# Two LayerNorms of a decoder layer: normalising on ScalarE, the bias on GpSimd, sums from the residual

## The chip, the core and the metric

The kernel runs on one core of a Trainium2 chip. It computes one whole decoder layer for 2048 tokens of width 1024 in one launch. The metric is the device time of an execution in microseconds (us). The engines of the core are TensorE (PE; PEld is its loading of weights), VectorE (DVE), ScalarE (ACT), GpSimd (POOL) and SyncE (SP), which issues most transfers.

## What is computed

The layer has two sub-layers: a token mixer of three head groups, and a mixture of experts (64 routed experts, eight for a token, and one shared expert). Behind each of them the residual stream is normalised; these two norms are what the change touches:

```python
def layer_norm(x, g, b):
    xf = x.astype(jnp.float32)
    mu = xf.mean(-1, keepdims=True)
    var = jnp.square(xf - mu).mean(-1, keepdims=True)
    return ((xf - mu) * lax.rsqrt(var + LN_EPS)).astype(x.dtype) * g + b

# each sub-layer:  x <- LayerNorm(ALPHA * x + gate * sublayer(x * (1 + scale) + shift))
```

All is float32, and the 2048 tokens are 16 blocks of 128 rows, a block's rows on the 128 partitions and its 1024 features along them.

## The kernel before

The input projection and the mixers, with the modulation rows, take up to about 1800 us of the profile. Then `phase_c` multiplies the mixers' output by the output projection and makes the **first norm**, a block of 128 rows at a time, and routes tokens to experts. The last phase, `moe_phase`, runs the experts; its end makes the **last norm** and writes the result. A scheduler lays out each engine's instructions, by the order of the code, priorities and its own estimates of durations, so that the code of several blocks is interleaved on every engine; what stands first in an engine's row waits for its inputs, and what is behind it waits as well.

**The first norm.** `tile_` (L1818) has five steps for each of the 16 blocks, and the loop over `t` advances three blocks in turn. For each half of 512 columns PE makes `po` (L1836), and VectorE makes the residual `r = ALPHA * x + po` (L1837) and takes `bn_stats` of it (L1840). `layer_norm_hat` (L1988) joins the two halves with `bn_aggr` (L1996), adds epsilon (L1998), takes the inverse root in `rsqrt` (L711 to L716: 11 tiny operations of VectorE, each reading the one before it) and makes the bias `lnnb` (L2001). ScalarE then normalises `r` in place (L2004). VectorE makes from it `h` and `h2p`, the experts' input (L1845, L1849), and the scaled residual (L1851, L1852). PE transposes `h2p` (L1860) and makes the router's scores (L1865). `route` (L1869) selects experts for the scores of four blocks at a time, of two at the very end; GpSimd's queue writes its gates `gt` (L1925) and counts (L1942). Both are small operations of VectorE. After the last block `rank_experts` (L1681) makes the tables that the experts need.

**The last norm.** In the last stage, from about 3620 us, the ten shared-expert units of `finish` (L2353) go one after the other: PE makes `py` (L2126, L2129), VectorE adds it to `a`, which is the routed experts' sum times the gate row (L2350), and takes the row sums `lnsu` with it (L2371). The six blocks whose shared-expert part was made earlier, SH0 = 6 (L1660), are mixed in between and get their sum on VectorE alone (L2366). Two blocks at a time then go through `norm` (L2320): the negative mean (L2327), squares and their sum on ScalarE (L2329), variance (L2332), `rsqrt`, and for each block two operations of VectorE over 128x1024, `(y + mean) * ln_g` (L2339) and `y * rs + ln_b` (L2340). Then SP sends the block out (L2341). The last block goes in two halves. `norm` is a generator, and `norms` (L2312) advances those under way before each unit. GpSimd has nothing to do in this stage.

Of the kernel before, what the change touches and what calls it, by code (L numbers as in the profile page):

```python
# [6 lines left out]
F32 = mybir.dt.float32  # L7
# [5 lines left out]
AF = mybir.ActivationFunctionType  # L13
ALU = mybir.AluOpType
AX = mybir.AxisListType
PSUM = bass.MemoryType.PSUM
P = 128
T = 2048
D = 1024
# [9 lines left out]
ALPHA = 2.0 ** 0.25  # L29
# [673 lines left out]
def rsqrt(nc, pool, x, shape, floor=None, name="rs"):  # L703

    V = nc.vector
    if floor is not None:
        V.tensor_scalar(x, x, floor, None, op0=ALU.max)
    t = pool.tile(shape, I32, name=name + "i")
    y = pool.tile(shape, F32, name=name + "y")
    a = pool.tile(shape, F32, name=name + "a")  # L710
    V.tensor_scalar(t, x.bitcast(I32), 1, None, op0=ALU.logical_shift_right)  # L711
    V.tensor_scalar(y.bitcast(I32), t, -1.0, float(0x5f3759df), op0=ALU.mult, op1=ALU.add)  # L712
    for _ in range(3):
        V.scalar_tensor_tensor(a, y, -0.5, y, op0=ALU.mult, op1=ALU.mult)  # L714
        V.tensor_tensor(a, a, x, op=ALU.mult)  # L715
        V.scalar_tensor_tensor(y, a, 1.5, y, op0=ALU.add, op1=ALU.mult)  # L716
    return y
# [1037 lines left out]
def phase_c(tc, A, g, S, mixT, modrow, C):  # L1755


    nc = tc.nc
    V, G, ACT, PE = nc.vector, nc.gpsimd, nc.scalar, nc.tensor
    woH, woL = C.wo  # L1760
    with ExitStack() as es:
# [3 lines left out]
        wk = pool("c_wk", 2)  # L1765
# [52 lines left out]
        def tile_(t, h2T):  # L1818
            t0 = t * P
            parts = C.first if t == 0 else []  # L1820
            load = mixed(nc, S, mx_ if t % 2 else C.mx, t, parts, G if t == 1 else nc.sync, V)
            if t:
                next(load)
            x = xp.tile([P, D], F32, name="x")
            nc.sync.dma_start(x, A["x"][0, t0:t0 + P, :])
            if t:
                next(load)
            mH, mL = parts
            yield
            r = rp.tile([P, D], F32, name="r")  # L1830
            for n in range(2):
                ps = C.pp.tile([P, CH], F32, name="po")
                sl = slice(n * 512, (n + 1) * 512)
                for k in range(KT):
                    for i, (a_, b_) in enumerate(((mH, woH), (mH, woL), (mL, woH))):
                        PE.matmul(ps, lhsT=a_[:, k, :], rhs=b_[:, k, sl], start=(k == 0 and i == 0), stop=(k == KT - 1 and i == 2))  # L1836
                V.scalar_tensor_tensor(r[:, sl], x[:, sl], ALPHA, ps, op0=ALU.mult, op1=ALU.add)  # L1837
                if n == 0:
                    st = sm.tile([P, 2, 6], F32, name="lnst", bufs=2)
                V.bn_stats(out=st[:, n, :], in_=r[:, sl])  # L1840
                yield
            xh = layer_norm_hat(tc, sm, r, r, st=st)
            yield
            h2 = wk.tile([P, D], F32, name="h2")
            V.tensor_tensor(h2, xh, bc["sc2"], op=ALU.mult)  # L1845

            hp = wk.tile([P, D], F32, name="h2p", bufs=3)
            cut = lambda a: a.rearrange("p (q k) -> p q k", k=KT)
            V.tensor_tensor(hp.rearrange("p (k q) -> p q k", k=KT), cut(h2), cut(bc["sh2"]), op=ALU.add)  # L1849
            h2 = hp  # L1850
            V.tensor_tensor(xh, xh, lng, op=ALU.mult)  # L1851
            V.tensor_tensor(xh, xh, lnb, op=ALU.add)  # L1852
            nc.sync.dma_start(S["x1"][t0:t0 + P, :], xh)
            nc.sync.dma_start(S["h2"][t0:t0 + P, 0:D], h2)
            yield
            hT = wk.tile([P, KT, P], F32, name="hT")
            for n in range(2):
                ps = pt.tile([P, CH], F32, name="tr")
                for k in range(4):
                    PE.transpose(ps[:, k * P:(k + 1) * P], h2[:, (4 * n + k) * P:(4 * n + k + 1) * P], g.ident)  # L1860
                ACT.activation(hT[:, 4 * n:4 * n + 4, :].rearrange("p a b -> p (a b)"), ps, AF.Copy)
            yield
            ps = pr.tile([P, CH], F32, name="rt")
            for k in range(KT):
                PE.matmul(ps[:, 0:NE], lhsT=hT[:, k, :], rhs=rw[:, k, :], start=(k == 0), stop=(k == KT - 1))  # L1865
            ACT.activation(h2T, ps[:, 0:NE], AF.Sigmoid)
            yield
# [117 lines left out]
        rank_experts(tc, g, S, cnt_e, sm, pr)  # L1985


def layer_norm_hat(tc, sm, out, r, parts=1, st=None):  # L1988

    nc = tc.nc  # L1990
    if st is None:
        st = sm.tile([P, 2, 6], F32, name="lnst")
        for n in range(2):
            nc.vector.bn_stats(out=st[:, n, :], in_=r[:, n * 512:(n + 1) * 512])
    mv = sm.tile([P, 2], F32, name="lnmv")
    nc.vector.bn_aggr(out=mv, in_=st)  # L1996
    va = sm.tile([P, 1], F32, name="lnva")
    nc.vector.tensor_scalar(va, mv[:, 1:2], 1e-5, None, op0=ALU.add)  # L1998
    y = rsqrt(nc, sm, va, [P, 1], None, "ln")
    nb = sm.tile([P, 1], F32, name="lnnb")  # L2000
    nc.vector.scalar_tensor_tensor(nb, mv[:, 0:1], -1.0, y, op0=ALU.mult, op1=ALU.mult)  # L2001
    for i in range(parts):
        c = slice(i * D // parts, (i + 1) * D // parts)
        nc.scalar.activation(out[:, c], r[:, c], AF.Identity, bias=nb, scale=y)  # L2004
    return out
NEAR = 4
NEAR2 = 5
# [6 lines left out]
def moe_phase(tc, A, g, S, modrow, out):  # L2014
    nc = tc.nc
    V, G, ACT, PE = nc.vector, nc.gpsimd, nc.scalar, nc.tensor
    with ExitStack() as es:
# [302 lines left out]
        def norm(blocks):  # L2320


            n = len(blocks)
            mean = sm.tile([P, 2], F32, name="lnmean")[:, 0:n]
            sq = sm.tile([P, 2], F32, name="lnsq")[:, 0:n]
            for i, (rows, y, su) in enumerate(blocks):
                V.tensor_scalar(mean[:, i:i + 1], su[:, 0:1], su[:, 1:2], -1.0 / D, op0=ALU.add, op1=ALU.mult)  # L2327
                junk = xg.tile([P, HC], F32, name="x")[:, 0:D]
                ACT.activation(junk, y, AF.Square, bias=mean[:, i:i + 1], accum_out=sq[:, i:i + 1])  # L2329
            yield  # L2330
            va = sm.tile([P, 2], F32, name="lnva")[:, 0:n]
            V.tensor_scalar(va, sq, 1.0 / D, 1e-5, op0=ALU.mult, op1=ALU.add)  # L2332
            rs = rsqrt(nc, sm, va, [P, n], None, f"ln{n}")
            yield
            for i, (rows, y, su) in enumerate(blocks):
                parts = 2 if rows.stop == T else 1
                for q in range(parts):
                    hs = slice(q * D // parts, (q + 1) * D // parts)
                    V.scalar_tensor_tensor(y[:, hs], y[:, hs], mean[:, i:i + 1], ln[0][:, hs], op0=ALU.add, op1=ALU.mult)  # L2339
                    V.scalar_tensor_tensor(y[:, hs], y[:, hs], rs[:, i:i + 1], ln[1][:, hs], op0=ALU.mult, op1=ALU.add)  # L2340
                    nc.sync.dma_start(out[rows, hs], y[:, hs])  # L2341
                yield

# [150 lines left out]
```

## Time and profile before

| what | us |
|---|---|
| time of the runs, median of 3 | 3731.58 (3721.93 to 3741.07) |
| the profiled execution | 3729.63 |
| its span, first to last instruction | 3727.9 |
| PE busy | 3439.3 (92%) |
| VectorE busy | 2640.9 (71%) |
| ScalarE busy | 1962.2 (53%) |
| GpSimd busy | 881.8 (24%) |

The shares are means over the whole span. What an edit is worth is read in its own stage, from the busy time in that stretch and from the wait that ends last there. The names behind a line are the tile written, an arrow, and the tiles read; the tile `w` in the last norm is the block `y`, and `wraw` is the row `ln_g` or `ln_b`, both kept in buffers that weights used earlier. In the first norm the norm's tiles are called `lnmv`, `lnva`, `lny`, `lnnb`.

### The profile page before, as it was taken

What the parts mean: (1) busy time and instruction counts of PE and PEld (TensorE: products, weight loads), DVE (VectorE), ACT (ScalarE), POOL (GpSimd) and SP (SyncE); (2) the same over time, 40 slices, a digit from 0 to 9 for tenths busy, and PEclk for the clock granted to TensorE, in tenths of its full rate; (3) what the DMA queues carried; (4) which work ended last, traced back from release to release, by engine and by line L of the source; (5) the groups of instructions that cost most, each with busy time, mean ns of one, the idle gap of its engine ahead of it and who ended that gap; (6) DMA issues with size and microseconds to landing.
All of it is one profiled execution on the core that took longest, in us unless ns stands there. A gap on an engine that the chain in (4) does not pass through costs nothing. (4 is left out here: it accounts for less than half of the span.)

```text
span 3727.9 us, 64046 instructions
## 1 busy us (share of the span) xinstructions
PE 3439.3 (92%) x23084; PEld 2985.7 (80%) x23084; DVE 2640.9 (71%) x6951; ACT 1962.2 (53%) x3471; POOL 881.8 (24%) x817
## 2 busy tenths in 40 slices
PE   7899999799999879999898799999999999999998
PEld 5677777688888767778787798998888888888996
DVE  6555899888888678888799545555556555556659
ACT  4243656355555567767322355555555555556642
POOL 1000000322223155543000022332223322232210
PEclk9999999899999889999999899999999999999999
DMA  7756466400000132222543478888889888888986
GB/s 251 232 199 221 150 211 226 162 26 25 20 24 18 30 105 79 84 66 78 170 149 140 146 206 232 242 232 233 244 244 242 244 236 234 236 234 256 290 237 215
DMA packets 276235, 640.38 MB, mean 172 GB/s; under 512 B 34428, under 2 KB 115364, under 8 KB 275784
## 3 DMA queue, kind: packets, MB, share of 16 engines
q1 hardware_dynamic: 231760, 481.09, 38.6%
q0 software_dynamic: 40832, 150.32, 18.2%
q10 hardware_dynamic: 3320, 4.83, 0.4%
q8 instruction: 183, 3.00, 0.3%
q14 instruction: 140, 1.15, 0.1%
HBM read 467.14 MB, written 169.00 MB: 171 GB/s over the span
## 5 line engine op out<-in xcount | busy, mean ns | idle before, releaser
L2112 PE MATMUL p<-hH,w 128*128 128x256 f32 (+8 forms) x4352 | 875.1, 289 | 9.3 <-DVE w L2060 6.6
L2112 PEld LDWEIGHTS p<-hH,w 128*128 128x128 f32 x4352 | 707.4, 191 | 18.9 <-DVE w L2060 6.9
L2060 DVE TENSOR_TENSOR w<-wraw,w 128x1024 fp32r<-128x1024 f32 x396 | 474.7, 1223 | 293.2 <-ACT w L2059 278.9
L2112 PE MATMUL p<-hL,w 128*128 128x256 f32 (+8 forms) x2176 | 617.2, 284 | 0.7 <-DVE hL L65 0.7
L2059 ACT ACTIVATE w<-wraw 128x1024 fp32r<-128x1024 f32 x396 | 406.2, 1054 | 234.5 <-DMA wraw<-in_exp_w_dram 112.2
L2166 POOL DMA_INDIRECT scratch_acc<-y,idx x157 | 262.3, 1671 | 782.6 <-ACT y L2165 312.8
L2129 PE MATMUL py<-w,gH 128*128 128x512 f32 (+5 forms) x1384 | 441.8, 401 | 2.0 <-ACT gH L62 1.6
L2112 PEld LDWEIGHTS p<-hL,w 128*128 128x128 f32 x2176 | 416.4, 191 | 6.5 <-DVE hL L65 0.9
L343 PE MATMUL pj<-hTH,w 128*128 128x512 f32 x1152 | 376.6, 402 | 16.6 <-ACT w L202 10.8
L65 DVE TENSOR_TENSOR hL<-tr,hH 128x512 fp32r<-128x512 f32 (+7 forms) x346 | 213.2, 627 | 210.8 <-ACT hH L62 197.6
L2129 PEld LDWEIGHTS py<-w,gH 128*128 128x128 f32 (+5 forms) x1384 | 236.6, 178 | 68.4 <-issue 8.1
L2165 ACT ACTIVATE y<-py,gt 128x512 f32<-128x512 f32 (+5 forms) x314 | 213.6, 683 | 145.9 <-PE py L2129 132.8
L343 PEld LDWEIGHTS pj<-hTH,w 128*128 128x128 f32 x1152 | 220.5, 193 | 70.8 <-ACT w L202 13.8
L62 ACT ACTIVATE hH<-tr 128x512 fp32r<-128x512 f32 (+7 forms) x346 | 184.3, 545 | 176.1 <-PE tr L2072 156.5
L2129 PE MATMUL py<-w,gL 128*128 128x512 f32 (+5 forms) x692 | 273.9, 396 | 0.6 <-DVE gL L65 0.5
L2140 POOL DMA_INDIRECT x<-scratch_h,idx x157 | 162.9, 1038 | 333.0 <-DVE L L2182 80.3
L343 PE MATMUL pj<-hTL,w 128*128 128x512 f32 x576 | 230.9, 401 | 0.0
L2072 PE MATMUL tr<-ident,x 128*128 128x128 f32 (+5 forms) x1384 | 191.9, 265 | 35.0 <-issue 17.9
L2072 PEld LDWEIGHTS tr<-ident,x 128*128 128x128 f32 (+5 forms) x1384 | 149.6, 140 | 46.0 <-issue 30.5
L2129 PEld LDWEIGHTS py<-w,gL 128*128 128x128 f32 (+5 forms) x692 | 122.9, 178 | 39.1 <-DVE gL L65 1.8
L2093 PE MATMUL p<-w,hH 128*128 128x256 f32 (+2 forms) x736 | 141.8, 289 | 0.0
L343 PEld LDWEIGHTS pj<-hTL,w 128*128 128x128 f32 x576 | 111.5, 194 | 23.5 <-issue 0.9
(626 smaller groups left out, 8152.0 us busy)
## 6 DMA issues: line engine op xcount, KB each, us to landing
wraw<-in_exp_w_dram SPq DMA_DIRECT2D x384, 512.0 KB
w<-scratch_wH SPq DMA_DIRECT2D x57, 512.0 KB
w<-scratch_wL SPq DMA_DIRECT2D x57, 512.0 KB
mw<-in_w_mod_dram SPq DMA_DIRECT2D x48, 512.0 KB
scratch_rw<-po SPq DMA_DIRECT2D x44, 256.0 KB
w<-in_w_in_dram SPq DMA_DIRECT2D x21, 512.0 KB
x<-in_x_dram SPq DMA_DIRECT2D x40, 256.0 KB
scratch_wH<-w SPq DMA_DIRECT2D x19, 512.0 KB
```

The lines of the kernel that those rows point to most:

```text
L62: nc.scalar.activation(hi, src, AF.Copy)
L65: (lo_eng or nc.vector).tensor_tensor(lo, src, hi.bitcast(F32), op=ALU.subtract)
L343: nc.tensor.matmul(ps, lhsT=a_[:, k, :], rhs=b_[k], start=(k == 0 and i == 0), stop=(k == KT - 1 and i == 2))
L2059: ACT.activation(wh[:, c], raw, AF.Copy)
L2060: V.tensor_tensor(wl[:, c], raw, wh[:, c].bitcast(F32), op=ALU.subtract)
L2072: PE.transpose(ps[:, k * n:(k + 1) * n], x[0:n, (4 * h + k) * P:(4 * h + k + 1) * P], g.ident[0:n, 0:n])
L2093: PE.matmul(ps[i][:n, 0:256], lhsT=(hH, hL)[a][:, k, 0:n], rhs=w[i][b][:, k, :], start=(k == 0 and j == 0), stop=(k == KT - 1 and j == 2))
L2112: PE.matmul(ps[i][:, 0:n], lhsT=w[i][a][:, k, m * P:(m + 1) * P], rhs=(hH, hL)[b][:, k, 0:n], start=(k == 0 and j == 0), stop=(k == KT - 1 ...
L2129: PE.matmul(ps[:n], lhsT=(gH, gL)[a][:, m, c:c + n], rhs=w[2][b][:, m, h * CH:(h + 1) * CH], start=(more is None and m == 0 and j == 0), s ...
L2140: G.indirect_dma_start(out=x[0:m, :], out_offset=None, in_=S["h2"], in_offset=bass.IndirectOffsetOnAxis(ap=ix[0:m], axis=0))
L2165: ACT.activation(y[:m, hs], ps[:m], AF.Copy, scale=gt[:m])
L2166: G.indirect_dma_start(out=S["acc"], out_offset=bass.IndirectOffsetOnAxis(ap=ix[0:m], axis=0), in_=y[0:m, :], in_offset=None, compute_op=A ...
```

## The change

In the first norm the two `bn_stats` and the `bn_aggr` of a block go. The residual's operation on VectorE now accumulates the row sum of each half (`accum_out`), one tiny operation makes the negative mean, and ScalarE squares the centred block with accumulation; the squares themselves go into the tile `h2`, which is overwritten later. The normalising by ScalarE stays.

In the last norm a tiny operation makes `nb = mean * rs` for the two blocks. ScalarE then normalises the block in place, VectorE multiplies by `ln_g`, and `ln_b` is added by GpSimd for blocks 0 to 13 and by VectorE for the last two. The transfer out waits for the addition.

```diff
@@ tile_
-                V.scalar_tensor_tensor(r[:, sl], x[:, sl], ALPHA, ps, op0=ALU.mult, op1=ALU.add)
                 if n == 0:
-                    st = sm.tile([P, 2, 6], F32, name="lnst", bufs=2)
-                V.bn_stats(out=st[:, n, :], in_=r[:, sl])
+                    su = sm.tile([P, 2], F32, name="lnsu", bufs=2)
+                V.scalar_tensor_tensor(r[:, sl], x[:, sl], ALPHA, ps, op0=ALU.mult, op1=ALU.add, accum_out=su[:, n:n + 1])
                 yield
-            xh = layer_norm_hat(tc, sm, r, r, st=st)
-            yield
             h2 = wk.tile([P, D], F32, name="h2")
+            xh = layer_norm_hat(tc, sm, r, r, su, h2)
+            yield
             V.tensor_tensor(h2, xh, bc["sc2"], op=ALU.mult)
@@ layer_norm_hat
-    nc.vector.bn_aggr(out=mv, in_=st)
+    nc.vector.tensor_scalar(mean, su[:, 0:1], su[:, 1:2], -1.0 / D, op0=ALU.add, op1=ALU.mult)
     va = sm.tile([P, 1], F32, name="lnva")
-    nc.vector.tensor_scalar(va, mv[:, 1:2], 1e-5, None, op0=ALU.add)
+    nc.scalar.activation(junk, r, AF.Square, bias=mean, accum_out=va)
+    nc.vector.tensor_scalar(va, va, 1.0 / D, 1e-5, op0=ALU.mult, op1=ALU.add)
     y = rsqrt(nc, sm, va, [P, 1], None, "ln")
     nb = sm.tile([P, 1], F32, name="lnnb")
-    nc.vector.scalar_tensor_tensor(nb, mv[:, 0:1], -1.0, y, op0=ALU.mult, op1=ALU.mult)
+    nc.vector.tensor_tensor(nb, mean, y, op=ALU.mult)
@@ norm
             rs = rsqrt(nc, sm, va, [P, n], None, f"ln{n}")
+            nb = sm.tile([P, 2], F32, name="lnnb")[:, 0:n]
+            V.tensor_tensor(nb, mean, rs, op=ALU.mult)
             yield
             for i, (rows, y, su) in enumerate(blocks):
+                ACT.activation(y, y, AF.Identity, bias=nb[:, i:i + 1], scale=rs[:, i:i + 1])
+                ended = rows.stop > T - 2 * P
                 parts = 2 if rows.stop == T else 1
                 for q in range(parts):
                     hs = slice(q * D // parts, (q + 1) * D // parts)
-                    V.scalar_tensor_tensor(y[:, hs], y[:, hs], mean[:, i:i + 1], ln[0][:, hs], op0=ALU.add, op1=ALU.mult)
-                    V.scalar_tensor_tensor(y[:, hs], y[:, hs], rs[:, i:i + 1], ln[1][:, hs], op0=ALU.mult, op1=ALU.add)
+                    V.tensor_tensor(y[:, hs], y[:, hs], ln[0][:, hs], op=ALU.mult)
+                    (V if ended else G).tensor_tensor(y[:, hs], y[:, hs], ln[1][:, hs], op=ALU.add)
                     nc.sync.dma_start(out[rows, hs], y[:, hs])
```

The scheduler also lays the instructions out anew. Two places follow. The first is VectorE in the last stage, near its end: before, the two passes of the last norm (L2339, L2340) over two blocks, beside the sums (L2371) of the next one.

```order
L2327 TENSOR_SCALAR lnmean<-lnsu 128x1
L2340 SCALAR_TENSOR_TENSOR w<-w,ln2y,wraw 128x1024 x2
L2332 TENSOR_SCALAR lnva<-lnsq 128x2
L2339 SCALAR_TENSOR_TENSOR w<-w,lnmean,wraw 128x1024
L2350 TENSOR_TENSOR x<-x,g2b 128x1024
L711 TENSOR_SCALAR ln2i<-lnva 128x2
L2371 SCALAR_TENSOR_TENSOR w,lnsu<-py,x 128x512
L712 TENSOR_SCALAR ln2y<-ln2i 128x2
L2371 SCALAR_TENSOR_TENSOR w,lnsu<-py,x 128x512
```

The same place after the change, where L2329 is now `nb`, L2337 the multiply, L2348 the gate row's multiply, L2369 the sum, L2321 the mean and L2326 the variance:

```order
L716 SCALAR_TENSOR_TENSOR ln2y<-ln2a,ln2y 128x2
L2329 TENSOR_TENSOR lnnb<-lnmean,ln2y 128x2
L2337 TENSOR_TENSOR w<-w,wraw 128x1024
L2348 TENSOR_TENSOR x<-x,g2b 128x1024
L2337 TENSOR_TENSOR w<-w,wraw 128x1024
L2369 SCALAR_TENSOR_TENSOR w,lnsu<-py,x 128x512 x2
L2093 TENSOR_TENSOR s<-s,p_48464 128x256
L2321 TENSOR_SCALAR lnmean<-lnsu 128x1
L2326 TENSOR_SCALAR lnva<-lnsq 128x1
```

The four passes of two blocks are two multiplies, and nothing stands between `nb` and the first of them, nor between a mean (L2321) and the variance (L2326) that needs ScalarE's squares. GpSimd has 14 additions (L2338) at the end of its row, behind its last transfer; ScalarE has one more 128x1024 operation (L2332) for each of the 16 blocks.

The second place is VectorE in the tail of `phase_c`, the last block of the first norm among the routing of the last two. Before, from the bias (L2001) on:

```order
L2001 SCALAR_TENSOR_TENSOR lnnb<-lnmv,lny 128x1
L1879 MAX top<-sel 128x8 x14
L1940 CAST cw<-before 64x1
L1882 TENSOR_TENSOR gs<-top 128x16
L1888 TENSOR_TENSOR gt<-gs 128x128
L1845 TENSOR_TENSOR h_28416<-r,bcsc_26220 128x1024
L1889 TENSOR_TENSOR eq<-gs 128x128
L1849 TENSOR_TENSOR h2p<-h_28416,bcsh_26218 128x128x8
```

After, with `lnnb` on L1997, the routing's `gt` on L1887 and the multiply by the modulation on L1844:

```order
L1881 TENSOR_TENSOR gs<-top 128x16
L1997 TENSOR_TENSOR lnnb<-lnmean,lny 128x1
L1887 TENSOR_TENSOR gt<-gs 128x128
L1888 TENSOR_TENSOR eq<-gs 128x128
L1889 TENSOR_TENSOR eq<-eq,glow 128x128
L1890 TENSOR_TENSOR gt<-gt,eq 128x128
L1892 TENSOR_REDUCE grank<-gt 128x16
L1844 TENSOR_TENSOR h_28378<-r,bcsc_26220 128x1024
L1893 TENSOR_SCALAR grank<-grank 128x16
```

Five more small routing operations (L1888 to L1892) now stand ahead of the block's `h` and `h2p`. Further ahead, `gt` of the blocks before these two (L1921, before L1922) and with it GpSimd's transfer of it moved in front of block 14's `h` (L1844), behind which it stood. Between these two places, in the routed experts' part, the order on every engine is as before.

## Rows read from the trace of the kernel before

**Rows 1.** The page's head and busy times: engine, us, share of the span, instructions.

```profile
span 3727.9 us, 64046 instructions
...
PE 3439.3 (92%) x23084; PEld 2985.7 (80%) x23084; DVE 2640.9 (71%) x6951; ACT 1962.2 (53%) x3471; POOL 881.8 (24%) x817
```

**Rows 2.** Last stage: stretch, its length, busy us per engine, PEclk, DMA share.

```profile
core 0: us, PE busy (x) PEld busy (x) DVE busy (x) ACT busy (x) POOL busy (x), PEclk, DMA share, GB/s
3621.30:3714.20 92.90, 86.04 (x509) 69.88 (x507) 91.61 (x230) 28.45 (x55) 0.00 (x0) 1.00 0.63 217
3621.30:3724.50 103.20, 86.04 (x509) 69.88 (x507) 101.31 (x264) 29.69 (x57) 0.00 (x0) 0.96 0.59 205
```

**Rows 3.** VectorE in the last stage: durations ns min/median/max, first to last start, forms.

```profile
L2339 DVE SCALAR_TENSOR_TENSOR w<-w,lnmean,wraw x17: 746/1279/1285, 3627.1 to 3720.5; 128x1024 f32<-128x1024 f32 x15, 128x512 f32<-128x512 f32 x2
```

**Rows 4.** VectorE at the end, in order: start us, us, operation.

```profile
3713.17 1.22 DVE L2350 TENSOR_TENSOR x<-x,g2b 128x1024 f32<-128x1024 f32 x1
3714.30 0.15 DVE L711 TENSOR_SCALAR ln1i<-lnva 128x1 int32<-128x1 int32 x1
3714.36 1.28 DVE L2339 SCALAR_TENSOR_TENSOR w<-w,lnmean,wraw 128x1024 f32<-128x1024 f32 x1
3715.56 0.15 DVE L712 TENSOR_SCALAR ln1y<-ln1i 128x1 int32<-128x1 int32 x1
...
3716.30 0.69 DVE L2371 SCALAR_TENSOR_TENSOR w<-py,x 128x512 f32<-128x512 f32 x1
...
3717.54 0.16 DVE L715 TENSOR_TENSOR ln1a<-ln1a,lnva 128x1 f32<-128x1 f32 x1
3717.73 0.16 DVE L716 SCALAR_TENSOR_TENSOR ln1y<-ln1a,ln1y 128x1 f32<-128x1 f32 x1
...
3723.09 1.41 DVE L2340 SCALAR_TENSOR_TENSOR w<-w,ln1y,wraw 128x512 f32<-128x512 f32 x2
```

**Rows 5.** ScalarE at the same place: the last sum of squares.

```profile
3717.33 1.15 ACT L2329 ACTIVATE x<-w,lnmean 128x1024 f32<-128x1024 f32 x1 [6.64 <-issue]
3718.38 0.19 ACT L2329 ACTIVATION_READ_ACCUMULATOR x<-w,lnmean 128x1 f32 x1
```

**Rows 6.** GpSimd subtracting two 128x1024 tiles: count, busy us, mean ns, idle before.

```profile
L65 POOL TENSOR_TENSOR mwl<-mw,mwh 128x1024 fp32r<-128x1024 f32 x32 | 77.3, 2414 | 37.7 <-ACT mwh L62 35.0 <-PE w L1446 2.8
```

**Rows 7.** Two VectorE lines in the mixer stage, durations as in 3.

```profile
L1540 DVE TENSOR_TENSOR mrow<-mrow,mb x8: 637/1322/2770, 1341.8 to 1693.8; 1x512 f32<-1x512 f32 x8
...
L1542 DVE TENSOR_TENSOR mrow<-mrow,w x24: 656/671/677, 1347.1 to 1723.9; 2x512 f32<-2x512 f32 x24
```

**Rows 8.** GpSimd about 1488 us, in order of time.

```profile
1488.04 2.40 POOL L65 TENSOR_TENSOR mwl<-mw,mwh 128x1024 fp32r<-128x1024 f32 x1 [1.91 <-ACT mwh L62]
```

**Rows 9.** VectorE at the same time.

```profile
1488.21 2.77 DVE L1540 TENSOR_TENSOR mrow<-mrow,mb 1x512 f32<-1x512 f32 x1
1490.91 0.67 DVE L1308 CUSTOM_DVE_ANT_0 L<-sc,Mq 128x512 f32<-128x512 f32 x1
```

**Rows 10.** Waits of the last stage: us in total, times, longest.

```profile
PE py L2126 <- DVE w L2371: 4.6, 3, 2.4
```

**Rows 11.** Attention's output stage and its end, columns as in 2.

```profile
1820.00:2018.00 198.00, 198.00 (x1035) 168.43 (x1034) 182.77 (x569) 49.91 (x69) 2.75 (x4) 1.00 0.42 145
2020.00:2024.00 4.00, 0.85 (x6) 0.74 (x6) 4.00 (x4) 0.22 (x1) 0.00 (x0) 0.90 0.92 349
2024.00:2040.00 16.00, 8.07 (x39) 7.34 (x38) 13.39 (x59) 3.63 (x6) 1.32 (x2) 0.50 0.69 247
```

**Rows 12.** First norm's operations, durations as in 3.

```profile
L1840 DVE BATCH_NORM_STATS2 lnst<-r x32: 672/686/696, 1809.2 to 2024.3; 128x6 f32<-128x512 f32 x32
...
L1996 DVE BATCH_NORM_AGGREGATE lnmv<-lnst x16: 186/203/209, 1810.6 to 2026.0; 128x2 f32<-128x12 f32 x16
...
L2004 ACT ACTIVATE r<-r,lnnb,lny x16: 1229/1243/1247, 1820.3 to 2030.8; 128x1024 f32<-128x1024 f32 x16
```

**Rows 13.** VectorE in the tail of that stage, with its wait in brackets.

```profile
2033.94 0.29 DVE L1888 TENSOR_TENSOR gt<-gs 128x128 f32<-128x128 f32 x1 [2.58 <-DMA scratch_h<-gt]
```

More of the change, by code (lines that the diff above doesn't have):

```diff
@@ L1836, in tile_ @@
                         PE.matmul(ps, lhsT=a_[:, k, :], rhs=b_[:, k, sl], start=(k == 0 and i == 0), stop=(k == KT - 1 and i == 2))
-                V.scalar_tensor_tensor(r[:, sl], x[:, sl], ALPHA, ps, op0=ALU.mult, op1=ALU.add)
                 if n == 0:
-                    st = sm.tile([P, 2, 6], F32, name="lnst", bufs=2)
-                V.bn_stats(out=st[:, n, :], in_=r[:, sl])
+                    su = sm.tile([P, 2], F32, name="lnsu", bufs=2)
+                V.scalar_tensor_tensor(r[:, sl], x[:, sl], ALPHA, ps, op0=ALU.mult, op1=ALU.add, accum_out=su[:, n:n + 1])
                 yield
-            xh = layer_norm_hat(tc, sm, r, r, st=st)
+            h2 = wk.tile([P, D], F32, name="h2")
+            xh = layer_norm_hat(tc, sm, r, r, su, h2)
             yield
-            h2 = wk.tile([P, D], F32, name="h2")
             V.tensor_tensor(h2, xh, bc["sc2"], op=ALU.mult)
@@ L1985, in phase_c, with layer_norm_hat @@
         rank_experts(tc, g, S, cnt_e, sm, pr)
-def layer_norm_hat(tc, sm, out, r, parts=1, st=None):
+def layer_norm_hat(tc, sm, out, r, su, junk):
     nc = tc.nc
[L1991 to L1995, printed above, removed]
-    nc.vector.bn_aggr(out=mv, in_=st)
+    mean = sm.tile([P, 1], F32, name="lnmean")
+    nc.vector.tensor_scalar(mean, su[:, 0:1], su[:, 1:2], -1.0 / D, op0=ALU.add, op1=ALU.mult)
     va = sm.tile([P, 1], F32, name="lnva")
-    nc.vector.tensor_scalar(va, mv[:, 1:2], 1e-5, None, op0=ALU.add)
+    nc.scalar.activation(junk, r, AF.Square, bias=mean, accum_out=va)
+    nc.vector.tensor_scalar(va, va, 1.0 / D, 1e-5, op0=ALU.mult, op1=ALU.add)
     y = rsqrt(nc, sm, va, [P, 1], None, "ln")
     nb = sm.tile([P, 1], F32, name="lnnb")
-    nc.vector.scalar_tensor_tensor(nb, mv[:, 0:1], -1.0, y, op0=ALU.mult, op1=ALU.mult)
-    for i in range(parts):
-        c = slice(i * D // parts, (i + 1) * D // parts)
-        nc.scalar.activation(out[:, c], r[:, c], AF.Identity, bias=nb, scale=y)
+    nc.vector.tensor_tensor(nb, mean, y, op=ALU.mult)
+    nc.scalar.activation(out, r, AF.Identity, bias=nb, scale=y)
     return out
```

## The prediction

> **What bounds the kernel now.** Over the whole span PE is the busiest engine [rows 1], but that share is a mean, and the change touches two stages with limits of their own. So I read the busy time in those two stretches first, then the order of operations inside them, then the waits.
>
> In the last stage VectorE works 101.31 of the 103.2 us from the first gate-row multiply to the last addition, PE 86.04 us of the same stretch, GpSimd none [rows 2]. VectorE is what paces it, and PE has some 7 us of slack up to its end at 3714.2, of which 4.6 us is waiting for VectorE's sum [rows 2, 10]. After PE's last product VectorE goes on alone for 10.3 us, and the last transfer ends 3.4 us behind VectorE (3727.9 against 3723.09 + 1.41) [rows 1, 4]. So here a microsecond of VectorE is a microsecond of the kernel, down to the point at which PE takes over.
>
> In the first norm's stage it is the other way round: from 1820 to 2018 PE is busy 198.00 of 198 us and VectorE 182.77 [rows 11]. What VectorE saves on the first 14 blocks or so is worth nothing. [...]
>
> **The last norm, VectorE's own work.** The two passes are 32 block-lengths: 15 whole blocks and two halves of L2339, and as many of L2340 [rows 3]. A pass lasts 1.28 us by its own record, but the next operation starts after 1.20 (3714.36 to 3715.56), and a plain multiply of two tiles, L2350, gives way after 1.13 (3713.17 to 3714.30) [rows 4]. I use these steps, since the queue is full. Removed: 32 x 1.20 = 38.4 us. Added: 16 multiplies x 1.13 = 18.1, the two last blocks' additions 2.3, nine `nb` (seven pairs, two singles) at about 0.15 = 1.3. That is 16.7 us less.
>
> **The additions on GpSimd.** No addition of the norm ran there before; the nearest row is GpSimd's subtraction of two tiles of the same 128x1024, 2.41 us, 32 times [rows 6]. 14 additions are 33.7 us, and GpSimd is otherwise idle in the stage, so its own time fits. The question is what VectorE does meanwhile. In the mixers' stage the trace has the answer: at 1488.04 GpSimd began such a subtraction, VectorE began L1540, which reads two SBUF tiles, at 1488.21, and it ended only at 1490.98, 2.77 us instead of the 0.64 of its shortest execution; GpSimd had ended at 1490.44 [rows 7 to 9]. VectorE lost 2.13 us. L1542 does the same arithmetic with one operand in PSUM and never took more than 0.677 [rows 7]. In the last stage VectorE's operations around a multiply mostly read two SBUF tiles (the gate row's multiply, the next block's multiply, the splits `gL` from SBUF, the sums of the six early blocks); the sums `y` of L2371 read PSUM. So the loss for an addition lies between 0 (VectorE happens to do PSUM operations or to wait) and 2.41 us, 0 to 33.7 in all. I take 1.75 us for 13 of them: somewhat under the 2.13 that one measured, because the order after the change has a PSUM operation or a tiny one directly behind some multiplies, and none for the last, behind which stand two sums from PSUM and a wait. 22.8 us.
>
> [...]
>
> **ScalarE in the chain.** Before, the two passes of one pair covered the squares of the next. Now a pair's mean, squares (1.15 + 0.19), variance, root, `nb`, ScalarE's normalising (about 1.24, as in L2004) and multiply stand in series [rows 5, 12]. In the new order nothing lies between a mean and its variance at four or five places, and between `nb` and its multiply at two. Uncovered these are worth up to 5 x 1.34 + 2 x 1.24 = 9.2 us; covered, 0. I take 6, nearer to the upper end because VectorE executes strictly in its order; part of this time lies under a running addition and is not paid twice. The ends: PE's `py` waits behind VectorE's sums, and SP's transfers of a block out now wait for GpSimd's addition with the loads of later blocks behind them; the slack of two or more blocks ahead covers that, and if it didn't, the price would be one addition, 2.41 us, for a block.
>
> The tail after the last sum (3716.30 + 0.69) is within these 6 us: the last block's squares are no longer behind the other block's pass, the root stays a chain at 0.195 us a step (3717.54 to 3717.73) [rows 4], the normalising of 1.24 comes in [rows 12], and two half passes are each a little shorter. Sum for the stage: -16.7 + 22.8 + 6 = **+12.1 us**.
>
> **The first norm.** For a block, two `bn_stats` and a `bn_aggr` go (0.69, 0.69, 0.20) [rows 12], a mean comes, and ScalarE gets 1.34 us of squares in the chain [rows 5]. ScalarE has room (49.91 of 198 us) [rows 11], and VectorE has the previous block's work to do while it squares. For the PE-bound blocks that is nothing either way. In the tail, VectorE is serial: I count off one `bn_stats` and the `bn_aggr`, 0.9 us, and the 2.58 us wait [rows 12, 13], because the gates' computation and with it GpSimd's transfer now stand ahead of block 14's `h` instead of behind it, some us earlier. The five routing operations ahead of the last `h` are only moved on the same engine. **-3.5 us**, between -7 (if the transposes that PE does at the lower clock also come earlier) and +2 (if the squares aren't covered and the wait stays). It is handed to the experts' start whole.
>
> **Sum.** +12.1 - 3.5 = +8.6: the profiled execution's 3729.63 becomes 3738.2. The median of the runs is 1.95 us above it, so about 3740. What a measurement of this kernel can tell from no change is about 0.5%, 18.7 us, so this is within it.
>
> **Rivals.**
>
> [...]
>
> B, slower by over 0.5%: every addition takes VectorE for its full 2.41 us and ScalarE's round trips are all bare: -16.7 + 33.7 + 9.2 - 3.5 = +22.7, 3754. It crosses the bound when the loss for an addition is over (18.7 + 3.5 + 16.7 - 9.2) / 14 = 2.1 us, which is just the 2.13 that was measured [rows 7 to 9]. PE then idles longer than the 2.4 us of its longest wait now [rows 10], and after the idle stretch at 2020 its clock was granted at .50 for 16 us [rows 11]; a fall of that kind over 10 us of products adds up to 10 us more, 3764. Against: PSUM operations and waits absorb some.
>
> C: the change doesn't give the first norm's 3.5 us, because the squares on ScalarE are in the last block's chain and the wait only moves to another transfer. Then +12.1, 3744.
>
> **How the numbers follow.** Forecast 0.50, A 0.17, B 0.20, C 0.13. Faster by over 0.5% needs more than A's floor gives, 0.03; slower by over 0.5% is most of B and a little of the forecast's upper end, 0.18; within, 0.79. The range goes from just below A, 3721, to a little above B without the clock, 3757.
>
> **What would show it.** In the last stage of the changed profile: VectorE operations with two SBUF inputs lasting 2 to 3.5 us while GpSimd adds (lock), with sums from PSUM at 0.68 as before; waits of VectorE for ScalarE of 1.2 to 1.4 us at a variance and a multiply; VectorE still at the end of the chain. [...] If PE's clock leaves 1.00 before its last product, B. In the tail at 2034 the 2.58 us wait must be gone and the tables 3 to 4 us earlier; if they aren't, C. I am wrong in kind if the last stage takes less than 97 us or the experts' phase between, whose order is unchanged, moves by more than a few us.

## The result, and the profile after

The changed kernel is slower: 3767.27 us (median of 5 runs, 3754.87 to 3767.76) against 3729.33 for the kernel before beside it, a ratio of 1.0083 with a 95% interval of 1.0065 to 1.0101. That is 24 to 38 us. The profiled execution took 3765.56 us, with a span of 3763.8.

The last stage, from the first gate-row multiply (L2348, at 3625.4) to the end of the span, takes 138.4 us where it took 106.6, so 31.8 us were lost in it. The busy times of that stretch up to VectorE's last operation, and of three pieces of it (columns as in [rows 2]):

```profile
3625.40:3760.30 134.90, 96.77 (x497) 74.78 (x495) 114.14 (x259) 47.31 (x73) 38.36 (x14) 0.86 0.45 158
3684.00:3688.00 4.00, 0.00 (x0) 0.00 (x0) 4.00 (x13) 0.00 (x0) 0.71 (x1) 0.99 0.61 213
3688.00:3692.00 4.00, 3.98 (x9) 2.54 (x10) 3.12 (x9) 3.19 (x4) 0.54 (x1) 0.58 0.86 305
3708.00:3714.00 6.00, 3.76 (x9) 1.88 (x8) 5.71 (x12) 3.16 (x6) 2.35 (x1) 0.53 0.75 259
```

VectorE is busy for 114.14 of 134.9 us; before it was 101.31 of 103.2 [rows 2]. So it works 12.8 us longer, though it has less to do, and stands for 20.8 us where it stood for 1.9. PE, at 86.04 us before, needs 96.77, at a granted clock of 0.86 where it was 0.96: PE stands idle up to 3688, and in the next 4 us the granted clock is 0.58; in the 6 us from 3708, 0.53. Two products of `py` take 2.07 us at 3688.02, and 1.13 at 3655.75, where the clock is 1.00.

GpSimd in order of time, four of its 14 additions (start us, us, operation):

```profile
3644.65 2.43 POOL L2338 TENSOR_TENSOR w<-w,wraw 128x1024 f32<-128x1024 f32 x1 [28.29 <-issue]
3648.32 2.39 POOL L2338 TENSOR_TENSOR w<-w,wraw 128x1024 f32<-128x1024 f32 x1 [1.24 <-DVE w L2337]
3659.76 2.41 POOL L2338 TENSOR_TENSOR w<-w,wraw 128x1024 f32<-128x1024 f32 x1 [9.05 <-DVE lnva L2326]
...
3724.71 2.39 POOL L2338 TENSOR_TENSOR w<-w,wraw 128x1024 f32<-128x1024 f32 x1 [11.96 <-DVE w L2337]
```

VectorE at the same times:

```profile
3644.76 2.34 DVE L716 SCALAR_TENSOR_TENSOR ln2y<-ln2a,ln2y 128x2 f32<-128x2 f32 x1
...
3648.76 3.03 DVE L2348 TENSOR_TENSOR x<-x,g2b 128x1024 f32<-128x1024 f32 x1
...
3659.93 2.26 DVE L712 TENSOR_SCALAR ln2y<-ln2i 128x2 int32<-128x2 int32 x1
...
3724.55 0.69 DVE L2369 SCALAR_TENSOR_TENSOR w<-py,x 128x512 f32<-128x512 f32 x1
...
3725.18 0.42 DVE L65 TENSOR_TENSOR gL<-tr,gH 128x256 fp32r<-128x256 f32 x1
3725.52 0.20 DVE L2321 TENSOR_SCALAR lnmean<-lnsu 128x1 f32<-128x1 f32 x1
3725.64 2.54 DVE L2337 TENSOR_TENSOR w<-w,wraw 128x1024 f32<-128x1024 f32 x1
```

This is the hold of [rows 7 to 9]; "the lock" is from here on the name for such a lengthening, and for nothing more. A step of the root over two numbers for each partition, 0.15 us elsewhere, lasts 2.34 us and ends when GpSimd's addition ends (3644.76 + 2.34 = 3647.10, 3644.65 + 2.43 = 3647.08); the gate row's multiply lasts 3.03 instead of 1.22, a root step at 3659.93 2.26. In the addition of 3724.71 one sees who is held and who isn't: the sum from PSUM (0.69) and the split of a PSUM tile (`gL`, the low part of a value that PE multiplies in two parts, 0.42) run through beside it, and so does the mean over one number for each partition (0.20); the multiply behind them, with two SBUF inputs, is held until 3727.1. In all, 13 operations are long, by 1.3 to 2.2 us, together by 26.1 us over the shortest of their kind. The one addition of the 14 that holds nobody is the last, at 3739.93, behind which VectorE has sums from PSUM.

GpSimd is held too. Five of its additions last 3.25 to 3.33 us and one 2.75, the other eight 2.35 to 2.43. The five began while VectorE was in a two-input operation over 128x1024:

```profile
3696.49 3.32 POOL L2338 TENSOR_TENSOR w<-w,wraw 128x1024 f32<-128x1024 f32 x1 [2.63 <-DVE w L2337]
```

```profile
3696.32 1.22 DVE L2348 TENSOR_TENSOR x<-x,g2b 128x1024 f32<-128x1024 f32 x1
3697.46 2.37 DVE L715 TENSOR_TENSOR ln2a<-ln2a,lnva 128x2 f32<-128x2 f32 x1
```

The gate row's multiply keeps its 1.22 us and the addition lasts 0.9 us longer; but VectorE's next operation, a root step, is then held for 2.2 us, until the addition ends at 3699.81. So it went all five times: VectorE's next operation lasted 2.1 to 2.2 us longer. Being first saved VectorE one operation here and cost it the next.

Waits of the stage (us in total, times, longest):

```profile
PE py L2120 <- DVE w L2369: 23.4, 6, 5.5
...
DVE lnva L2326 <- ACT x L2323: 8.4, 7, 1.7
DVE w L2337 <- ACT w L2332: 4.9, 7, 1.4
...
DVE w L2369 <- PE py L2123: 3.1, 2, 1.8
```

VectorE waits 13.3 us for ScalarE, at the variance (L2326) and at the multiply (L2337); before, it waited for ScalarE once in the whole stage, 0.5 us. And PE waits 23.4 us for VectorE's sums, 5.5 us at the longest, where it was 4.6 and 2.4 [rows 10]. The end of VectorE's row shows the round trips bare, that is with no other work to cover them:

```profile
3752.47 0.21 DVE L2321 TENSOR_SCALAR lnmean<-lnsu 128x1 f32<-128x1 f32 x1
3753.99 0.15 DVE L2326 TENSOR_SCALAR lnva<-lnsq 128x1 f32<-128x1 f32 x1 [1.31 <-ACT x L2323]
...
3756.31 0.16 DVE L2329 TENSOR_TENSOR lnnb<-lnmean,ln1y 128x1 f32<-128x1 f32 x1
3757.84 1.29 DVE L2337 TENSOR_TENSOR w<-w,wraw 128x512 f32<-128x512 f32 x2 [1.37 <-ACT w L2332]
3759.05 1.29 DVE L2338 TENSOR_TENSOR w<-w,wraw 128x512 f32<-128x512 f32 x2
```

The variance behind the mean waits 1.31 us for the squares, then the eleven root operations and `nb` stand 0.19 us apart with nothing beside them, then the first half's multiply waits 1.37 us for the normalising.

The first norm's stage is shorter. Before, the output projection's products (L1836) and the copy of the permutation with which the experts' part can begin (the third figures are the first and the last start):

```profile
L1836 PE MATMUL po<-woH,mH x256: 387/389/794, 1750.1 to 2017.7; 128*128 128x512 f32 x128
...
2065.36 0.18 DVE L1712 COPY perm<-k_pc 128x64 f32<-128x64 f32 x1
```

After, with the group comparison (L1887) between them:

```profile
L1836 PE MATMUL po<-woH,mH x256: 388/390/767, 1754.3 to 2021.3; 128*128 128x512 f32 x128
...
2030.91 0.29 DVE L1887 TENSOR_TENSOR gt<-gs 128x128 f32<-128x128 f32 x1
...
2061.90 0.17 DVE L1712 COPY perm<-k_pc 128x64 f32<-128x64 f32 x1
```

From the last block's products to the permutation it took 47.7 us (2017.7 to 2065.36), now 40.6 (2021.3 to 2061.90); the comparison no longer waits [rows 13].

### The profile page after: what moved, and what is told of

Its sections match the earlier page's. It is cut to its first block, busy times and chain, and to the rows that moved or that the text cites. A ratio compares the mean times of both kernels' runs of the same rounds, so it can differ in the third digit from the quotient of the medians.

```text
span 3763.8 us, 64107 instructions
## 1 busy us (share of the span) xinstructions
PE 3454.8 (92%) x23084; PEld 2992.6 (80%) x23084; DVE 2642.4 (70%) x6946; ACT 2000.1 (53%) x3519; POOL 918.6 (24%) x831
## 5 line engine op out<-in xcount | busy, mean ns | idle before, releaser
L2123 PE MATMUL py<-w,gH 128*128 128x512 f32 (+5 forms) x1384 | 452.7, 409 | 2.7 <-ACT gH L62 1.8
L343 PE MATMUL pj<-hTH,w 128*128 128x512 f32 x1152 | 376.2, 402 | 17.4 <-ACT w L202 12.3
```

Of the source, the lines that this page charges most:

```text
L343: nc.tensor.matmul(ps, lhsT=a_[:, k, :], rhs=b_[k], start=(k == 0 and i == 0), stop=(k == KT - 1 and i == 2))
L2123: PE.matmul(ps[:n], lhsT=(gH, gL)[a][:, m, c:c + n], rhs=w[2][b][:, m, h * CH:(h + 1) * CH], start=(more is None and m == 0 and j == 0), s ...
```

## The experiments

All were run beside the kernel before. "Stage" is the stretch from the first gate-row multiply to the end of the span: 106.6 us before, 138.4 after. An operation is "long" when it lasts over 0.5 us more than the shortest of its kind in the stage. Kernels that ran once are compared by the stage, because the stretches ahead of it scatter: the first gate-row multiply came between 3610.6 and 3635.1 us in these profiles. In the last stage VectorE and ScalarE have the order of the kernel before (first norm alone, additions alone, fills, one-input operations, gate tile), or that of the changed kernel (last norm alone). Where additions are left out or moved to VectorE, or the multiply is moved, the scheduler orders the work anew.

**The first norm alone.** The last norm stays as before; the diff is that of the change without `norm`.

> Only the first norm is changed; the last norm is that of the kernel before. In the changed kernel the permutation copy that starts the experts' part came at 2061.90 us instead of 2065.36, 3.5 us earlier, but the first gate-row multiply of the last stage came at 3625.4 instead of 3621.3, so some 7.6 us were lost in between, where no instruction was moved. Theory 1: the first norm gains 3.5 us by itself and the 7.6 us are the scatter of the experts' part from run to run; the last stage (first gate-row multiply to the end of the span) stays at 106.6 us, the time is 0 to 7 us under before. Theory 2: the earlier start of the experts' part costs those 7.6 us each time; the first gate-row multiply then comes again at about 3625, and the time is 3 to 5 us over before.

Measured: ratio 0.9975 (0.9953 to 0.9997), 3723.29 us median of 10 runs against 3737.46. The stage is that of before, with VectorE busy 101.41 of 103.40 us:

```profile
3610.60:3714.00 103.40, 86.37 (x512) 70.20 (x510) 101.41 (x264) 29.69 (x57) 0.00 (x0) 0.96 0.58 206
```

From the last products to the permutation it took 40.6 us. From the permutation to the first gate-row multiply it took 1553.9 us; this stretch took 1555.9 before, 1563.5 after, and between 1552.9 and 1566.1 in the kernels below, with the old first norm as with the new. Theory 1 holds: the 7.6 us of the expectation are scatter of the experts' part, and the sign that the prediction had set for being wrong in kind, an experts' phase that moves, was this scatter.

**The last norm alone.** The first norm stays as before.

> Only the last norm is changed; the first norm is that of the kernel before. Theory: the whole loss lies here. The last stage (first gate-row multiply to the end of the span) lasts 138 us, as in the changed kernel, against 106.6 before, and the time is 30 to 35 us over before. Rival: part of the loss (some 6 us) belongs to the first norm's effect on the experts' part; then the time is 25 us over before or less, with the stage at 138 all the same.

Measured: ratio 1.0094 (1.0058 to 1.0130), stage 138.3 us, 13 long operations with 25.8 us in excess. The time, 22 to 49 us over before by the interval, does not exclude the rival's 25 us; the stage, which loses 31.7 us of the changed kernel's 31.8, and the first norm alone, which loses nothing, do. The whole loss lies here.

**No addition.** The other half of the question: what is left of the loss if the addition costs nothing at all? The kernel leaves `ln_b` out for blocks 0 to 13.

```diff
-                    (V if ended else G).tensor_tensor(y[:, hs], y[:, hs], ln[1][:, hs], op=ALU.add)
+                    if ended:
+                        V.tensor_tensor(y[:, hs], y[:, hs], ln[1][:, hs], op=ALU.add)
```

> The changed kernel without GpSimd's 14 additions: ln_b is left out for blocks 0 to 13, all else stands. In the changed kernel 13 VectorE operations lasted 1.3 to 2.2 us too long while GpSimd added, 26.1 us in all, and VectorE waited 13.3 us for ScalarE and 5.1 us for PE. Theory 1 (the lock is the main cost): the long operations are gone, the last stage falls from 138.4 to 105 to 112 us, and what is left over the floor of PE is the waits for ScalarE. Theory 2 (the round trip through ScalarE is the main cost, the lock mostly lies beside it): the stage stays at 125 us or more.

Measured: one execution of 3726.27 us, stage 107.8 us. No VectorE operation is long. The stage's busy times and VectorE's waits for ScalarE:

```profile
3616.80:3721.10 104.30, 85.94 (x500) 69.61 (x498) 89.07 (x259) 47.56 (x73) 0.00 (x0) 0.94 0.57 204
```

```profile
DVE lnva L2326 <- ACT x L2323: 7.0, 8, 1.6
...
DVE w L2337 <- ACT w L2332: 4.8, 6, 1.4
```

Theory 1 holds: 30.6 us lie between this and the changed kernel. VectorE's operations stand in another order here, so that difference is not the lock's alone. The run also says something that neither theory had asked: with 14 additions removed altogether the stage is still not shorter than before. VectorE is busy 12.2 us less (89.07 against 101.31) and gives it all back standing idle. In the order that it got, the split over ScalarE is worth nothing, even with a free addition.

**Additions alone.** The kernel before with GpSimd's additions put in, for nobody to read:

```diff
                     V.scalar_tensor_tensor(y[:, hs], y[:, hs], rs[:, i:i + 1], ln[1][:, hs], op0=ALU.mult, op1=ALU.add)
+                    if rows.stop <= T - 2 * P:
+                        G.tensor_tensor(idle, y, ln[1], op=ALU.add)
```

> The kernel before, with 14 additions on GpSimd put in (the finished block 0 to 13 plus ln_b into a tile that nobody reads), each behind the second pass of its block. The order on PE, VectorE, ScalarE and SyncE is word for word that of the kernel before. Theory (lock): VectorE's operations with two SBUF inputs that overlap an addition last some 2 us longer, 12 to 14 times, and since VectorE paces the stage the last stage grows from 106.6 by 20 to 30 us. [...]

Measured: ratio 1.0093 (1.0058 to 1.0127), stage 137.1 us. The stage's busy times, then GpSimd and VectorE at the first two additions:

```profile
3616.80:3750.50 133.70, 96.78 (x503) 75.95 (x502) 130.00 (x264) 29.34 (x57) 43.02 (x14) 0.87 0.45 158
```

```profile
3634.47 2.38 POOL L2343 TENSOR_TENSOR idle<-w,wraw 128x1024 f32<-128x1024 f32 x1 [26.36 <-DVE w L2341]
3638.08 2.42 POOL L2343 TENSOR_TENSOR idle<-w,wraw 128x1024 f32<-128x1024 f32 x1 [1.23 <-DVE w L2341]
```

```profile
3634.63 3.30 DVE L2341 SCALAR_TENSOR_TENSOR w<-w,ln2y,wraw 128x1024 f32<-128x1024 f32 x1
...
3638.19 2.34 DVE L2333 TENSOR_SCALAR lnva<-lnsq 128x2 f32<-128x2 f32 x1
```

VectorE is busy 130.00 us where it was 101.31. 14 operations are long, by 28.6 us together: the second pass of the next block lasts 3.30 us instead of 1.28, a variance over 128x2 2.34 instead of 0.17. The additions alone, with VectorE's and ScalarE's rows otherwise word for word the same, cost the stage 30.5 us, nearly what the whole change costs it, and the excess of the long operations accounts for 28.6 of them. This is the cleanest proof of the lock here, since the additions are all that was put in.

**All additions on VectorE.**

```diff
-                    (V if ended else G).tensor_tensor(y[:, hs], y[:, hs], ln[1][:, hs], op=ALU.add)
+                    V.tensor_tensor(y[:, hs], y[:, hs], ln[1][:, hs], op=ALU.add)
```

> The changed kernel with all 16 additions on VectorE, so that GpSimd has nothing in the last stage. Without the 14 additions the stage lasted 107.8 us, of which VectorE waited 12 us. Theory 1 (VectorE's row is strict, the waits for ScalarE stay): 14 x 1.13 = 15.8 us come on top, 120 to 124 us. Theory 2 (the additions fill the holes in which VectorE waits for ScalarE): 108 to 113 us. In both it is shorter than the 138.4 us with GpSimd's additions, since VectorE pays 1.13 us for its own addition and 2.0 for GpSimd's.

Measured: one execution of 3747.97 us, stage 120.1 us, no long operation. VectorE's waits for ScalarE:

```profile
DVE lnva L2326 <- ACT x L2323: 6.2, 5, 1.6
...
DVE w L2337 <- ACT w L2332: 3.5, 5, 1.4
```

It still waits 9.7 us for ScalarE, against 11.8 without the additions: they went mostly behind the waits, not into them, and theory 1 holds. On VectorE the 14 additions cost 12.3 us of stage, on GpSimd 30.6. Neither place makes the stage shorter than the 106.6 us of before.

**Half of the additions.** Even blocks on GpSimd, odd ones on VectorE.

> The changed kernel with seven of the 14 additions on GpSimd (the even blocks), the others on VectorE. All 14 on GpSimd: last stage 138.4 us, 26.1 us of lock in 13 operations; none: 120.1 us. Theory (each addition has its own price): about 7 long operations, 12 to 15 us of lock, stage 126 to 132 us. Rival (the loss is not proportional, for instance because PE's lower clock sets it): under 123 or over 136 us.

Measured: one execution of 3763.56 us, whose stage began 9.7 us later than in the changed kernel; stage 126.7 us, seven long operations, 14.9 us. This lies between the two ends, as the theory has it; each addition has its own price of about 2.1 us.

**The multiply ahead of the root.** VectorE's pass no longer needs what ScalarE makes:

```diff
-                    V.tensor_tensor(y[:, hs], y[:, hs], ln[0][:, hs], op=ALU.mult)
-                    (V if ended else G).tensor_tensor(y[:, hs], y[:, hs], ln[1][:, hs], op=ALU.add)
+                    V.scalar_tensor_tensor(y[:, hs], y[:, hs], mean[:, i:i + 1], ln[0][:, hs], op0=ALU.add, op1=ALU.mult)
+                    if ended:
+                        V.scalar_tensor_tensor(y[:, hs], y[:, hs], rs[:, i:i + 1], ln[1][:, hs], op0=ALU.mult, op1=ALU.add)
+                    else:
+                        ACT.activation(y[:, hs], y[:, hs], AF.Copy, scale=rs[:, i:i + 1])
+                        G.tensor_tensor(y[:, hs], y[:, hs], ln[1][:, hs], op=ALU.add)
```

> The changed kernel with another split of the last norm: VectorE makes (y + mean) * ln_g before the root, ScalarE then only multiplies by rs, GpSimd adds ln_b (the last two blocks: as in the kernel before). VectorE no longer waits for ScalarE's normalising, and its pass again covers the next squares. Theory (two separate costs, the lock and the bare round trips): the lock of about 26 us stays, the waits for ScalarE fall from 15.3 to under 4 us, the last stage falls from 138.4 to 115 to 127 us. Rival (the lock alone sets the stage, waits lie beside it): 135 us or more.

Measured: one execution of 3752.34 us, stage 126.1 us, 12 long operations with 21.8 us. VectorE's waits for ScalarE:

```profile
DVE lnva L2326 <- ACT x L2323: 4.0, 3, 1.4
...
DVE w L2334 <- ACT x L2323: 3.2, 6, 0.9
```

The stage is inside the range of the theory, but the lock did not stay at 26 us, and the waits fell from 15.3 only to 7.7 us with small ones at a split, not under 4: the pass (L2334) overwrites the tile that the squares read, and in the new order it waits for them. The stage is 12.3 us shorter while the lock is only 4.3 us smaller, so the waits are a cost of their own; what is left of them was again taken too low.

**Fills and one-input operations.** Which GpSimd work holds VectorE? The kernel before, with ten operations on the used-up tile `a`, once `G.memset(a, 0.0)` and once a multiply in place:

```diff
                     V.scalar_tensor_tensor(y[:, hs], ps, 1.0, a[:, hs], op0=ALU.mult, op1=ALU.add, accum_out=su[:, q:q + 1])
+                G.tensor_scalar(a, a, 2.0, None, op0=ALU.mult)
```

> The kernel before, with ten fills on GpSimd put in: the tile a of each of the ten shared-expert blocks is set to zero (128x1024) as soon as VectorE has added it, and nobody reads it after. The order on the other engines is word for word that of the kernel before. A fill writes SBUF and reads nothing. Theory 1 (the conflict is over the read side, as VectorE's two inputs suggest): no VectorE operation is longer, the last stage stays at 106.6 us within 1.5. Theory 2 (any GpSimd operation on SBUF holds VectorE): ten VectorE operations are longer by most of a fill, the stage grows by 5 us or more.

Measured: one execution of 3739.67 us, stage 106.8 us. VectorE is as busy as before, 101.35 us. The stage's busy times, two of the ten fills, and VectorE during them:

```profile
3631.10:3734.50 103.40, 87.35 (x509) 70.94 (x507) 101.35 (x264) 29.68 (x57) 9.54 (x10) 0.95 0.58 205
```

```profile
3646.57 0.95 POOL L2372 MEMSET x<- 128x1024 f32 x1 [9.41 <-issue]
...
3706.83 0.96 POOL L2372 MEMSET x<- 128x1024 f32 x1 [6.90 <-DVE ln2y L716]
```

```profile
3646.57 0.15 DVE L716 SCALAR_TENSOR_TENSOR ln2y<-ln2a,ln2y 128x2 f32<-128x2 f32 x1
...
3646.77 0.15 DVE L714 SCALAR_TENSOR_TENSOR ln2a<-ln2y 128x2 f32<-128x2 f32 x1
...
3706.72 1.22 DVE L2350 TENSOR_TENSOR x<-x,g2b 128x1024 f32<-128x1024 f32 x1
```

Root steps of 128x2 and a whole gate-row multiply run beside a fill at their usual 0.15 and 1.22 us. Theory 1 holds: a fill, which only writes, held none of the two-input operations that it met. No `tensor_scalar` over 128x2 met one.

> As the fills, but each of the ten GpSimd operations multiplies the tile a by 2 in place: the same place, shape and writes, and one SBUF input read. GpSimd's 128x1024 one-input operation took 1.13 us in the mixers' stage. Theory 1 (a read of one input is enough for the lock): some ten VectorE operations are longer by 0.5 to 1.0 us, the last stage grows by 5 to 10 us over 106.6. Theory 2 (only GpSimd's two-input operations hold VectorE): it stays within 1.5 us.

Measured: one execution of 3742.29 us, stage 112.5 us, VectorE busy 107.01 us. One of the ten, and the operation that it held:

```profile
3643.86 2.77 POOL L2372 TENSOR_SCALAR x<-x 128x1024 f32<-128x1024 f32 x1 [7.80 <-issue]
```

```profile
3644.01 0.89 DVE L714 SCALAR_TENSOR_TENSOR ln2a<-ln2y 128x2 f32<-128x2 f32 x1
3644.94 0.16 DVE L715 TENSOR_TENSOR ln2a<-ln2a,lnva 128x2 f32<-128x2 f32 x1
```

Theory 1 holds, with a surprise in the sizes. GpSimd's operation lasts 2.77 us by its record, not the expected 1.13, but the root step that met it was held for 0.74 us only (0.89 against 0.15) and the next ones ran beside the rest of it. Seven operations are long, by 0.73 to 0.84 us, 5.4 us in all: five root steps and two passes.

**A gate tile of its own.** The wait of [rows 13] taken away by itself, in the kernel before:

```diff
-            gate = sm.tile([P, TPC, NE], F32, name="gt")[:, 0:B]
+            gate = sm.tile([P, TPC, NE], F32, name="gate")[:, 0:B]
```

> The kernel before, with one change: the gates of the routing get a tile of their own instead of sharing gt with the group comparison, so that the comparison (L1888) no longer waits for GpSimd's transfer of the gates. The order on every engine is that of the kernel before. From the first transpose of h2p to the permutation copy the kernels with the old first norm took 231 us, those with the new one 224. Theory 1 (the wait is 2.6 of the 7 us, as the prediction counted it): 228 to 229 us. Theory 2 (the wait covers something that is late anyway, and the 7 us come from the new order): 230.5 us or more.

Measured, the output projection, the comparison, the operation behind it and the permutation copy:

```profile
L1836 PE MATMUL po<-woH,mH x256: 389/389/792, 1762.4 to 2030.1; 128*128 128x512 f32 x128
...
2043.77 0.29 DVE L1888 TENSOR_TENSOR gt<-gs 128x128 f32<-128x128 f32 x1
2044.48 1.23 DVE L1845 TENSOR_TENSOR h<-r,bcsc 128x1024 f32<-128x1024 f32 x1 [0.42 <-ACT r L2004]
...
2075.69 0.18 DVE L1712 COPY perm<-k_pc 128x64 f32<-128x64 f32 x1
```

The comparison runs at once, and `h` now waits 0.42 us for ScalarE. From the first transpose to the permutation 229.1 us; from the last products 45.6 instead of 47.7. The wait is worth 2.1 us, and theory 1 holds for this part; the time of this one execution, 3737.17 us, can't show so little.

> The new first norm alone (last norm as before), with the same gate tile of its own; the order on every engine is that of the first norm alone. There the comparison no longer waits for the transfer. Expectation by both theories: the stretch from the first transpose to the permutation copy stays at 224 us within 0.5, and the time is that of the first norm alone, about 7 us under before (0.2%); a gain of over 2 us more would show that the shared tile still costs something.

Measured: ratio 0.9981 (0.9963 to 0.9999), 3726.72 us median of 12 runs against 3735.16; 224.1 us from the first transpose, 40.6 from the last products. The new order has no such wait to remove. This and the first norm alone are the two versions that beat the kernel before, by about 0.2%, with both intervals ending just short of no change.

## Why the prediction was wrong

The direction and the main mechanism were as forecast, slower by a lock that GpSimd's additions put on VectorE. The time was not: +8.6 us, upper end 3757, against some 31.

**VectorE's own work, -16.7 us.** Right for the long passes, but the small operations were missing. In the kernel without additions VectorE is busy 12.2 us less, not 16.7. Most of the other 4.5 us are small operations: a root step that slips in beside a long operation costs 0.06 us of VectorE's row (3714.30 to 3714.36 in [rows 4]), one that stands among its like 0.195. Take away the long passes and the root stands bare: the 99 root operations take 12.1 us of the row before and 15.5 without the additions, summed from one start to the next over the two timelines, and the means and variances a little over 1 us more.

**ScalarE in the chain, +6 us.** This is the step that failed. Without additions the stage is 107.8 us where -16.7 and nothing else would give 89.9. So 17.9 us stand where the sum had 6: 4.5 are the operations just named, and 13.4 are VectorE standing idle, 15.2 us (104.30 - 89.07) against 1.9 before, 11.8 of it in waits for ScalarE. That is over twice the 6 I took and well over the 9.2 I gave as the upper end. I counted five bare means and two bare normalisings, at the places that I looked at, and took all others as covered. In the changed profile VectorE waits at seven variances and at seven multiplies, 13.3 us; only three of these variances and two of these multiplies have nothing in front of them, and the others wait although one to four operations stand there. Before, each of the nine variances had at least one whole pass between it and its mean, and none waited. I should have asked what covers each of the nine pairs and singles once the two passes, which were the cover, are gone.

**The lock, 1.75 us for 13 additions = 22.8 us.** Nearly right in itself: 13 long operations, 26.1 us, 2.0 apiece, one addition free, for the reason given. The sum left out what follows from it: the late sums make PE wait, its granted clock falls (0.86 over the stretch against 0.96, 0.58 behind a wait of 5.2 us), and VectorE then waits for PE and for a split (3.1 us and 2.0 us). Against the kernel without additions, whose order differs, the stage is 30.6 us longer (138.4 - 107.8); in the kernel before with additions alone, whose order doesn't, 14 of them cost 30.5 us.

**The first norm, -3.5 us.** Right in kind, half in size: seven kernels with the new first norm take 40.6 to 40.8 us from the last products to the permutation, the kernel before 47.7, so -7.0, the lower end that I gave. (Four other kernels with the old norm take 47.3 to 49.9, with a wait of 2.3 to 4.5 us for the gates' transfer.) That wait is 2.1 of the 7.0. The other 5 us come with the rest of the edit: no `bn_stats` and no `bn_aggr` on VectorE behind the last residual, and `h2p` and one more pass of block 14 ahead of it; I counted only the first. Of the routing operations that moved ahead of the last `h` there are four (L1888, L1889, L1890, L1892), not five. How the 5 us divide between less work and order was not tried.

**The rivals.** C, no gain in the first norm, is out. A, at 0.17, was the chance of additions that cost VectorE nothing. No run shows it, nor the floor of A from which the lower end of the range, 3721, was taken: the kernel without any addition on GpSimd has a stage 1.2 us longer than before, since the waits for ScalarE (11.8 us there) stand in VectorE's row whether VectorE is full or not. Six of the 14 additions did last well over 2.41 us, but where VectorE was first, the addition waited for that one operation and then held the next. B is nearest to what came, including the falling clock; its point of 2.1 us for an addition was not reached (26.1 / 14 = 1.9), and the bound was still crossed, because the 9.2 us in its formula should have been 17.9; with these and the first norm's 7.0 the point is (18.7 + 7.0 + 16.7 - 17.9) / 14 = 1.75.

**The sum again.** From the changed kernel's own rows the stage is -16.7 for the passes, +26.1 for the lock, +3.3 for the rest of VectorE's busy time, mostly small operations, and +18.9 of standing idle (20.8 us against 1.9; 15.3 of the 20.8 in waits for ScalarE, 3.1 for PE): +31.6 of the measured +31.8. The prediction had +12.1. With -7.0 for the first norm this is +24.8, the lower end of the measured interval. The two profiles differ by more, 35.9 us, since the mixers' part and the experts' part, in which no instruction moved, were 3.6 and 7.6 us longer in this execution; such stretches differ by as much between kernels that don't differ in them. The range should have gone at least to 3764, the figure with the clock that stands under B: the measured ratio on the median of 3731.58 that was known gives 3762.6, and the median of the changed kernel's own runs, 3767.27, lies beyond both.

## What to carry to other kernels

An idle engine is free only if its work doesn't hold the busy one. Before a two-input operation goes to GpSimd, look in the trace for a VectorE operation that overlapped such a one, and charge its excess for each time; here that was more than the operation's own time on VectorE (2.0 us lost for 1.13 saved). When long operations are moved off a full engine, list what they were covering, place by place; their cover can be worth as much as their time (here 17.9 us against 16.7), and the kernel without the moved work is the cheapest way to see it.

## What the runs showed of the hardware

**Who holds whom.** Additions on GpSimd, which read two tiles in SBUF, held two-input VectorE operations on SBUF down to 128x2, for up to 2.2 us, and with them `tensor_scalar` operations over 128x2 with one input (2.1 us at 3659.93, above). With half of the additions and with the multiply ahead of the root, two-input root steps over 128x1 were held as well (2.30 us at 3742.41 and 1.74 us at 3731.77). A sum (0.69 us) and a split (0.42 us) with a PSUM operand, and a `tensor_scalar` over 128x1 (0.20 us), ran through beside the addition at 3724.71. Ten fills of 128x1024 on GpSimd, 0.95 us each, held nothing that they met.

**GpSimd's one-input operations.** A multiply by a constant was recorded at 2.77 us and held VectorE for 0.73 to 0.84 us only, so a GpSimd operation's recorded length is not always the time of the lock; why, these runs don't show. The 2.77 us themselves go with the form in this program: with one operation, the second argument of `tensor_scalar` left `None`, GpSimd took 2.77 us over 128x1024 and 5.40 us over 128x2048 (L167), and with two operations 1.04 us (L885) and 1.13 us (L1284) over 128x1024, and 1.99 and 2.82 us over 128x2048 (L1284); the lines are those of the changed kernel.

**PE's clock.** In the changed kernel the granted clock was lower in the 4 us behind the longest waits of PE for VectorE's sums: 0.58 behind 4.0 us that ended at 3629.95, 0.50 behind 4.8 us (3671.51), 0.58 behind 5.2 us (3688.02) and 0.50 behind 5.5 us (3740.51). It was 1.00 behind a wait of 1.7 us that ended at 3655.75. The length of the wait alone doesn't decide it: behind 2.2 us that ended at 3707.45 the clock was 0.62, and 0.53 over 3708 to 3714, while a wait of 2.4 us in the kernel before left it at 1.00 [rows 2, 10]. What else decides it, these runs don't show.
